# Moving the second heads' scaled copy of a row into the place of the next head's raw bias values

## The chip, the cores and the metric

The kernel runs on one core of a Trainium2 chip. The metric is the device time of one execution in microseconds. Lower is better. The core's engines are called as in the profile: PE (TensorE matmul), PEld (its weight loads), DVE (VectorE), ACT (ScalarE), POOL (GpSimd) and SP (SyncE, which here only issues DMAs). Each engine works through its own queue in order and waits there for what the others owe it.

## The reference, cut to what matters

One encoder layer on 1024 tokens of width 1024, all in float32. A combined projection feeds two kinds of attention heads. Group A is eight sliding-window heads. Group B, the "second heads", is eight heads of neighbourhood attention on a 16 x 64 grid of tokens: each token attends to a window of 8 x 16 tokens, with a learned bias for every offset in two dimensions.

```python
def row(args):                                   # one grid row of queries, group B
    q_r, r = args
    rs = jnp.clip(r - kh // 2, 0, rows - kh)
    k_rows = lax.dynamic_slice_in_dim(kg, rs, kh, axis=1)
    v_rows = lax.dynamic_slice_in_dim(vg, rs, kh, axis=1)
    ...
    bias = rpb32[:, row_off][:, :, col_off]
    s = jnp.einsum('bchd,bicjhd->bhcij', q_r, k_win) * scale + bias[None]
    p = jax.nn.softmax(s.reshape(B, B_HEADS, GRID_W, kh * NA_KW), axis=-1)
    return jnp.einsum('bhcij,bicjhd->bchd', p, v_win)
```

Behind both groups stand a norm of each group, an output projection with a residual, a gated MLP with a depthwise convolution, and a final norm.

## The kernel before

The tokens of the grid are put in an order in which a second head has eight blocks of 128 queries, called rows 0 to 7 here, and each block attends to itself and its neighbours: 384 keys, or 256 for rows 0 and 7. The heads are called 0 to 7. PE's order is written out by hand: between the matmuls of attention stand those of the projections and of the output projection of group A (the "filler", tiles `pj`), and the scores of a row are made two to three pairs of rows ahead of their use. The other engines' order is set by a scheduler from priorities and from which buffer is free.

A row goes through these steps. PE makes scores (L439). DVE adds the bias tile `xb` and takes the extreme, into a buffer `p` (L469). ACT takes the exponential and its sum (L473), and DVE the reciprocal `sm` (L474). From there a row takes one of two paths, by the string `QQTQQQTQ` of `PATH_B`:

- Rows 2 and 6 are T rows: POOL scales `p` in place (L477), PE transposes it (L501), ACT and DVE split the result into two float16 parts in the tile `turned` (L504, L505).
- The six others are Q rows: ACT writes the scaled high part into a staging tile, `hl` or one of two called `stage` (L488); POOL makes a scaled copy `y` (L493) and subtracts the high part from it, into the staging tile (L494); SP issues a DMA that transposes both parts into `turned` (L495, called the flip).

PE then multiplies `turned` with the values (L604); row 4's tile is first used in the chunk that follows the transposes of row 6.

The bias tile of the next head is begun at row 4 of the head before. A DMA on SP loads the raw values `rr` (L551), and two POOL operations turn them and the mask into `xb` (L562, L563). `rr` has one buffer of 489 float32 values per partition. POOL may do this no earlier than row 2's L477 ("scaled"). The pool `p` has six buffers; before the change it holds both the probability tiles `p` and the copies `y`, so that a Q row takes two of the six. POOL also subtracts the high parts of projection weights (L157, tile `wlo`).

Of the kernel before, what the change touches and what calls it, by code (L numbers as in the profile page):

```python
# [13 lines left out]
F32 = mybir.dt.float32  # L14
# [23 lines left out]
TURNED, PS, HLS, SPARE_A, LOWS = 3, 6, 1, (2, 5), 1  # L38
# [13 lines left out]
RAW_LEN = RPB_W * (ROWS - 1) + 24  # L52
# [11 lines left out]
def hybrid_layer(tc, xT, w_in, w_out, w_gate, w_up, w_down, small, sink, rpb, consts, rope, out):  # L64
    nc = tc.nc
    with ExitStack() as ctx:
# [8 lines left out]
        apool = inner("att", 2)  # L75
# [367 lines left out]
        apart = lambda ap: ap.rearrange("p (c w) -> p c w", w=128)  # L443
# [3 lines left out]
        def staged():  # L447
            if not stage:
                t = big("stage", "op").bitcast(F16)
                stage.extend(apool.tile([128, 3, 2, 128], F16, name="hl", tag=f"hl{i}", bufs=1) for i in range(HLS))  # L450
                stage.extend(t[:, 768 * i:768 * i + 768].rearrange("p (c s w) -> p c s w", s=2, w=128) for i in range(2))
            stage.append(stage.pop(0))
            return stage[-1]

        class Rows:
# [5 lines left out]
            def softmax(self, path, j, ps, n, bias, nsink=None, skip=0):  # L461

                c = n // 128
                with tc.high_priority(offset=50):
                    p = apool.tile([128, 386], F32, name="p", tag="p", bufs=PS)
                    nm, sm = (spool.tile([128, 1], F32, name=x) for x in ("nm", "sm"))
                    if nsink is not None:
                        nc.gpsimd.tensor_copy(p[:, n:n + 1], nsink)
                    nc.vector.tensor_tensor_reduce(  # L469
                        out=apart(p[:, 0:n]), in0=apart(ps[:, 0:n]), in1=bias, scale=1.0, scalar=3e38 if nsink is None else nsink,  # L470
                        op0=ALU.add, op1=ALU.min, accum_out=nm)
                    e = n if nsink is None else n + 1
                    nc.scalar.activation(p[:, 0:e], p[:, 0:e], AF.Exp, bias=nm, scale=-1.0, accum_out=sm)  # L473
                    nc.vector.reciprocal(sm, sm)  # L474
                    x = apart(p[:, 0:n])
                    if path in "PT":
                        mark["scaled"] = nc.gpsimd.tensor_scalar(x, x, sm, P_TOP, op0=ALU.mult, op1=ALU.mult)  # L477
                    if path == "T":
                        return lambda: self.turn(j, p, c, skip)
                    hl = staged()  # L480
                    hi, lo = (hl[:, 0:c, s] for s in range(2))
                    if path == "P":
                        nc.scalar.activation(hi, x, AF.Copy)
                        nc.gpsimd.tensor_tensor(lo, x, hi, op=ALU.subtract)
                    else:
                        by = spool.tile([128, 1], F32, name="by")
                        nc.vector.tensor_scalar(by, sm, P_TOP, None, op0=ALU.mult)
                        nc.scalar.activation(hi, x, AF.Copy, scale=by)  # L488
                        if path == "D":
                            nc.vector.scalar_tensor_tensor(lo, x, by, hi, op0=ALU.mult, op1=ALU.subtract)  # L490
                        else:
                            y = apart(apool.tile([128, 384], F32, name="y", tag="p", bufs=PS, padded_shape=[128, 386])[:, 0:n])
                            nc.gpsimd.tensor_scalar(y, x, sm, P_TOP, op0=ALU.mult, op1=ALU.mult)  # L493
                            nc.gpsimd.tensor_tensor(lo, y, hi, op=ALU.subtract)  # L494
                    mark["flip"] = nc.sync.dma_start(self.tile[:, j, skip:skip + c].rearrange("p i s q -> p (i s) q"), hl[:, 0:c], transpose=True)  # L495
# [1261 lines left out]
        for i, (p, j, c) in enumerate(order):  # L1757
# [4 lines left out]
            f, n = PARTS[c]  # L1762
# [148 lines left out]
```

## Time and profile before

| | |
|---|---|
| time, median of 3 runs | 1028.34 us (1028.22 to 1029.49) |
| time of the profiled execution | 1027.81 us |
| its span, first to last instruction | 1026.0 us |
| mean granted TensorE clock | 0.997 |
| PE busy | 1009.7 us (98%) |
| DVE busy | 875.6 us (85%) |
| ACT busy | 676.3 us (66%) |
| POOL busy | 216.4 us (21%) |
| second heads on PE, first to last use of `turned` | 190 to 344 us of the span |

The time of an execution is a little longer than its span, by 1.8 us here. PE is busy nearly all the time, so what the kernel takes is what PE does plus what PE waits. POOL's share is low over the whole span, but nearly all of its work lies in the first third, where the heads are. The change concerns the stretch of the second heads alone, from 186 to 346 us.

### The profile page before, as it was taken

Reading aid. Unit: us, or ns where it says so; the run is one execution under the profiler, and the core shown is the slowest. Engines: PE = TensorE matmul, PEld = TensorE weight load, DVE = VectorE, ACT = ScalarE, POOL = GpSimd, SP = SyncE. Lnnn points to the kernel's source line nnn. Section 1 sums busy time; section 2 is a strip of 40 time slices with the busy share of each in tenths; the row PEclk is TensorE's granted clock in tenths of the full one; section 3 lists DMA queues with packets and bytes.
Section 4 is the critical chain, followed back from the end, with each engine's and each line's share of the span. In section 5 each row is a group of like instructions: output and inputs, shape, how many; then the busy total and the mean of one; then the engine's idle time right before and its main releaser. Section 6 shows DMA issues by size and latency. Waiting matters only on the chain.

```text
span 1026.0 us, 15565 instructions
## 1 busy us (share of the span) xinstructions
PE 1009.7 (98%) x5102; PEld 577.8 (56%) x5102; DVE 875.6 (85%) x1714; ACT 676.3 (66%) x1242; POOL 216.4 (21%) x339
## 2 busy tenths in 40 slices
PE   9999999999999999999999999999999999999997
PEld 7877777777775545544444444444444444444446
DVE  6799988767898899999897988788888888999875
ACT  8667787768687687645777777754634666655551
POOL 2235455877866210001000000000000000000002
PEclk9999999999999999999999999999999999999998
DMA  8556564787799875201787767633232788978744
GB/s 314 198 133 139 115 138 106 159 155 137 136 195 216 280 255 171 82 1 42 251 279 251 266 230 256 232 114 134 82 114 103 256 263 291 309 245 269 250 147 165
DMA packets 143938, 191.79 MB, mean 187 GB/s; under 512 B 77360, under 2 KB 88112, under 8 KB 143856
## 3 DMA queue, kind: packets, MB, share of 16 engines
q1 hardware_dynamic: 133264, 164.84, 55.9%
q10 hardware_dynamic: 10592, 25.95, 6.6%
q8 instruction: 40, 0.66, 0.3%
q14 instruction: 42, 0.34, 0.1%
HBM read 132.81 MB, written 28.57 MB: 157 GB/s over the span
## 4 chain that ended last, share of the span: by engine, by line
PE 65%; DVE 2%; DMA 1%; ACT 1%; issue 0%; POOL 0%; DVEq 0%; ACTq 0%; POOLq 0%
PE dn L1199 6%; PE dn L1200 6%; PE dn L1201 6%; PE pj L180 6%; PE z L1200 5%; PE z L1201 5%; PE z L1199 5%; PE y L1200 4%; PE y L1201 4%; PE y L1199 4%; PE x L1199 4%; PE x L1200 4%; PE x L1201 4%; PE ss L1239 1%; DMA turned<-stage 1%; DVE wlo L1174 0%
## 5 line engine op out<-in xcount | busy, mean ns | idle before, releaser
L1201 PEld LDWEIGHTS <-wlo 128*128 128x128 f16 x898 | 87.8, 98 | 101.2
L1199 PEld LDWEIGHTS <-whi 128*128 128x128 f16 x898 | 88.0, 98 | 100.3
L1200 PEld LDWEIGHTS <-whi 128*128 128x128 f16 x898 | 87.8, 98 | 100.3
L1201 PE MATMUL dn<-xd,wlo 128*128 128x512 f16 (+1 forms) x330 | 120.5, 365 | 0.0
L1200 PE MATMUL dn<-xd,whi 128*128 128x512 f16 (+1 forms) x330 | 120.5, 365 | 0.0
L1199 PE MATMUL dn<-xd,whi 128*128 128x512 f16 (+1 forms) x330 | 120.5, 365 | 0.0
L172 PE MATMUL pj<-xgh,whi 128*128 128x512 f32 x248 | 106.9, 431 | 0.0
L1201 PE MATMUL z<-hg,wlo 128*128 128x512 f16 x264 | 100.2, 379 | 0.0
L1199 PE MATMUL z<-hg,whi 128*128 128x512 f16 x264 | 100.2, 379 | 0.0
L1200 PE MATMUL z<-hg,whi 128*128 128x512 f16 x264 | 100.2, 379 | 0.0
L174 PE MATMUL pj<-xgh,wlo 128*128 128x512 f32 x248 | 97.7, 394 | 0.0
L173 PE MATMUL pj<-xgl,whi 128*128 128x512 f32 x248 | 97.6, 393 | 0.0
L473 ACT ACTIVATE p<-p,nm 128x385 f32<-128x385 f32 (+3 forms) x128 | 74.7, 584 | 34.6 <-DVE nm L469 28.6
L1173 ACT ACTIVATE whi<-ws,m 128x512 f16<-128x512 f32 (+1 forms) x96 | 65.8, 708 | 37.7 <-DVE ws L1340 22.9
L1174 DVE SCALAR_TENSOR_TENSOR wlo<-ws,m,whi 128x512 f16<-128x512 f32 (+1 forms) x96 | 70.3, 742 | 18.3 <-ACT whi L1173 18.1
L1054 POOL TENSOR_TENSOR back<-back,cst 128x4 f32<-128x4 f32 (+1 forms) x7 | 2.8, 395 | 356.8 <-DVE back L1053 356.8
L1188 ACT ACTIVATE scan<-scan 128x1024 f32<-128x1024 f32 (+1 forms) x60 | 61.1, 1018 | 18.4 <-DMA scan<-in_w_down_dram 13.2
L1173 ACT ACTIVATE whi<-raw,m 128x512 f16<-128x512 f32 (+1 forms) x78 | 51.1, 699 | 16.8 <-DMA raw<-in_w_down_dram 10.1
L1174 DVE SCALAR_TENSOR_TENSOR wlo<-raw,m,whi 128x512 f16<-128x512 f32 (+1 forms) x78 | 55.5, 733 | 6.7 <-ACT whi L1173 6.6
L1201 PE MATMUL y<-hg,wlo 128*128 128x512 f16 x160 | 60.7, 379 | 0.0
L1200 PE MATMUL y<-hg,whi 128*128 128x512 f16 x160 | 60.7, 379 | 0.0
L1199 PE MATMUL y<-hg,whi 128*128 128x512 f16 x160 | 60.7, 379 | 0.0
(296 smaller groups left out, 2464.7 us busy)
## 6 DMA issues: line engine op xcount, KB each, us to landing
xd<-x SPq DMA_DIRECT2D x77, 256.0 KB, 5.3
raw<-in_w_down_dram SPq DMA_DIRECT2D x64, 256.0 KB, 3.3
x<-c ACTq DMA_DIRECT2D x22, 512.0 KB, 4.2
scan<-in_w_gate_dram SPq DMA_DIRECT2D x18, 512.0 KB, 4.7
scan<-in_w_up_dram SPq DMA_DIRECT2D x18, 512.0 KB, 5.5
raw<-in_w_gate_dram SPq DMA_DIRECT2D x18, 512.0 KB, 3.5
raw<-in_w_up_dram SPq DMA_DIRECT2D x18, 512.0 KB, 3.6
raw<-in_w_in_dram SPq DMA_DIRECT2D x32, 256.0 KB, 3.2
```

The source lines that it names most:

```text
L172: nc.tensor.matmul(ps, w[0], x[0][:, tsl(h)], start=first, stop=False)
L173: nc.tensor.matmul(ps, w[0], x[1][:, tsl(h)], start=False, stop=False)
L174: nc.tensor.matmul(ps, w[1], x[0][:, tsl(h)], start=False, stop=last)
L180: nc.tensor.matmul(ps, a, b, start=i == 0 and b is x[h][0] and a is w[0], stop=i == len(ws) - 1 and a is w[1])
L473: nc.scalar.activation(p[:, 0:e], p[:, 0:e], AF.Exp, bias=nm, scale=-1.0, accum_out=sm)
L1173: mark["whi"] = nc.scalar.activation(hi, src, AF.Copy, scale=by)
L1174: nc.vector.scalar_tensor_tensor(lo, src, by, hi, op0=ALU.mult, op1=ALU.subtract)
L1188: nc.scalar.activation(t, t, AF.Square, accum_out=dst)
L1199: nc.tensor.matmul(ps, w[0], x[0], start=first and i == 0, stop=False, skip_group_check=True)
L1200: nc.tensor.matmul(ps, w[0], x[1], start=False, stop=False, skip_group_check=True)
L1201: nc.tensor.matmul(ps, w[1], x[0], start=False, stop=last and i == len(ws) - 1, skip_group_check=True)
L1239: nc.tensor.matmul(narrow[h][:, c:c + 1], s2[:, c * 128:(c + 1) * 128], ones[:, 0:1], start=c == 0 and d == ADDED[h] - 1, stop=d == KT - 1 ...
```

## The change

The copy `y` of a Q row of the second heads no longer comes from the six buffers of the pool `p`. It takes the single buffer `rr`, padded to that buffer's length, which between two heads holds the raw bias values.

```diff
                         else:
-                            y = apart(apool.tile([128, 384], F32, name="y", tag="p", bufs=PS, padded_shape=[128, 386])[:, 0:n])
+                            y = apart(apool.tile([128, 384], F32, name="y", tag="rr", bufs=1, padded_shape=[128, RAW_LEN])[:, 0:n])
                             nc.gpsimd.tensor_scalar(y, x, sm, P_TOP, op0=ALU.mult, op1=ALU.mult)
                             nc.gpsimd.tensor_tensor(lo, y, hi, op=ALU.subtract)
```

Since the buffer is one, its tenants follow each other in the order in which the program asks for it: the copies of rows 0, 1 and 3 of a head, then the raw values of the next head, then the copies of rows 4, 5 and 7. PE's order is the same row for row. POOL, SP, DVE and ACT have the same instructions in another order.

On POOL, head 4, before: behind row 2's L477 come the bias tile, row 3, row 4 and row 5, one weight part, and row 6's L477.

```order
L477 TENSOR_SCALAR p<-p,sm 128x384 [waits DVE_49]
L562 TENSOR_TENSOR xb<-cst,rr 128x384 [waits DMAHW0_49]
L563 TENSOR_TENSOR xb<-cst,rr 128x2x128
L493 TENSOR_SCALAR y<-p,sm 128x384 [waits DVE_49]
L354 TENSOR_TENSOR gains<-par,up 128x1 [waits DVE_49]
L908 TENSOR_TENSOR gains<-gains,mix_up 128x4 [waits Pool_49]
L494 TENSOR_TENSOR stage<-y,stage 128x3x128 [waits DMAHW1_49,Activation_49]
L493 TENSOR_SCALAR y<-p,sm 128x384 [waits DVE_49]
```

After:

```order
L477 TENSOR_SCALAR p<-p,sm 128x384 [waits DVE_49]
L493 TENSOR_SCALAR y<-p,sm 128x384 [waits DVE_49,Pool_49]
L354 TENSOR_TENSOR gains<-par,up 128x1 [waits DVE_49]
L908 TENSOR_TENSOR gains<-gains,mix_up 128x4 [waits Pool_49]
L494 TENSOR_TENSOR stage<-y,stage 128x3x128 [waits DMAHW0_49,Activation_49]
L562 TENSOR_TENSOR xb<-cst,rr 128x384 [waits DMAHW7_49]
L563 TENSOR_TENSOR xb<-cst,rr 128x2x128
L493 TENSOR_SCALAR y<-p,sm 128x384 [waits DVE_49,Pool_49]
```

The bias tile has moved from ahead of row 3 to between row 3 and row 4. Behind these rows follow, in both, the rest of row 4 and row 5, the weight part, and row 6's L477. In head 5 that L477 stands between row 4's L493 and L494 after the change.

On SP, head 4, before: the raw values for head 6 are asked for as soon as the bias tile of head 5 is made, ahead of the flips of rows 3 and 4.

```order
L551 DMA rr<-in_rpb_dram 128x1x489 [waits Pool_49]
L495 DMA_TRANSPOSE turned<-stage 128x6x128 [waits DMAHW0_49,PE_49,Pool_49]
L495 DMA_TRANSPOSE turned<-stage 128x6x128 [waits DMAHW1_49,PE_49,Pool_49]
L382 DMA_TRANSPOSE v<-vhl 128x16x64 [waits DMAHW2_49,DVE_49]
L382 DMA_TRANSPOSE v<-vhl 128x16x64 [waits DMAHW3_49]
```

After:

```order
L495 DMA_TRANSPOSE turned<-stage 128x6x128 [waits PE_49,Pool_49]
L551 DMA rr<-in_rpb_dram 128x1x489 [waits DMAHW7_49]
L382 DMA_TRANSPOSE v<-vhl 128x16x64 [waits DMAHW0_49,DVE_49]
L382 DMA_TRANSPOSE v<-vhl 128x16x64 [waits DMAHW1_49]
L495 DMA_TRANSPOSE turned<-stage 128x6x128 [waits DMAHW2_49,PE_49,Pool_49]
```

The load of the raw values for head 5 itself now stands right behind row 3's flip. In head 3 the load stands ahead of row 3's flip and waits for POOL itself.

On DVE the scores of the next row (L469) have moved ahead of small or bulk work in several places, because a `p` buffer is free earlier. In head 5, before:

```order
L474 RECIPROCAL sm<-sm 128x1 [waits Activation_49]
L201 TENSOR_TENSOR mg<-mixa,mg 128x2x512
L487 TENSOR_SCALAR by<-sm 128x1 [waits DVE_49]
L469 ISA p,nm<-s,xb 128x384 [waits PE_49]
L469 ISA nm 128x1
```

After:

```order
L474 RECIPROCAL sm<-sm 128x1 [waits Activation_49]
L469 ISA p,nm<-s,xb 128x384 [waits PE_49,Pool_49]
L469 ISA nm 128x1
L487 TENSOR_SCALAR by<-sm 128x1 [waits DVE_49]
L201 TENSOR_TENSOR mg<-mixa,mg 128x2x512
```

Row 4's scores are read ahead of L201, which splits a tile of group A's output for the projection.

## The prediction

> **What bounds the kernel now.** I read the page first, then the stretch of the second heads by windows, then PE's waits in it, then the rows of POOL, PE and SP around row 4 of each head.
>
> ```profile
> PE 1009.7 (98%) x5102; PEld 577.8 (56%) x5102; DVE 875.6 (85%) x1714; ACT 676.3 (66%) x1242; POOL 216.4 (21%) x339
> 186.00:346.00 160.00, 157.82 (x894) 115.30 (x893) 124.56 (x354) 114.21 (x254) 116.94 (x143) 1.00 0.82 167
> PE o L604 <- DMA turned<-stage: 1.1, 2, 0.9
> PE o L604 <- DMA turned<-hl: 0.5, 1, 0.5
> PE pt L501 <- POOL p L477: 0.4, 1, 0.4
> ```
>
> PE bounds the kernel. In the stretch that the change touches it is busy 157.8 of 160 us, and its waits are 2.2 us, nearly all for finished rows. So there is at most 2.2 us to gain here, and every microsecond that a row comes later than PE's hand-written order asks for it is lost in full: PE's order is the same after the change, and the stages behind are PE's too. POOL is the fuller neighbour: 116.9 of 160 us.
>
> **What the change removes and adds.** No instruction is added. Six copies per head (48 in all) leave the pool `p`. That gives DVE a free `p` buffer earlier. In PE's waits above none is for DVE's reading of scores, so the removal is worth at most a part of the 2.2 us; DVE's new order brings row 4 of head 5 forward past one L201, and I count this inside the lag below.
>
> What it adds is one chain per head, for heads 0 to 6. Before, the raw values of a head were in place a whole head early, and the bias tile cost POOL only its own two operations. Now the raw values may be loaded only when row 3's subtraction has read the copy that stands in their place, and row 4's copy may be made only when the bias tile has read the raw values. POOL works in order, so it stands still meanwhile with rows 4, 5 and 6 behind it. The prices, one step after the other:
>
> ```profile
> L495 SPq DMA_TRANSPOSE turned<-stage x31: 1188/1220/1982, 190.2 to 339.7; - x31
> DMA to landing us min/median/max: 2.4/3.4/5.7
> rr<-in_rpb_dram SPq DMA_DIRECT2D x8, 244.5 KB, 4.7
> DMA to landing us min/median/max: 4.3/4.7/5.9
> L562 POOL TENSOR_TENSOR xb<-cst,rr x8: 979/986/1515, 38.9 to 313.0; 128x384 f32<-128x384 f32 x8
> L563 POOL TENSOR_TENSOR xb<-cst,rr x8: 707/734/1697, 39.9 to 314.0; 128x256 f32<-128x256 f32 x8
> L493 POOL TENSOR_SCALAR y<-p,sm x48: 474/584/1555, 181.1 to 338.5; 128x384 f32<-128x384 f32 x32, 128x256 f32<-128x256 f32 x16
> L494 POOL TENSOR_TENSOR stage<-y,stage x31: 668/913/1494, 189.2 to 339.0; 128x384 f16<-128x384 f32 x16, 128x256 f16<-128x256 f32 x15
> L477 POOL TENSOR_SCALAR p<-p,sm x16: 577/586/1110, 186.4 to 337.9; 128x384 f32<-128x384 f32 x16
> ```
>
> The first landing row is that of the flips, the second that of the raw values. From the end of row 3's subtraction: 1.3 us in which SP issues row 3's flip (1.22) and turns to the load; 4.7 to its landing; 1.7 for the bias tile (0.99 + 0.73); 1.5 for row 4 (0.58 + 0.91); 1.5 for row 5; 0.6 for row 6's L477. Together 11.3 us to the end of L477, and 9.2 to the end of row 4's subtraction, which a flip of 3.4 us follows. In head 3 the load goes ahead of the flip: 1.3 less.
>
> How long PE leaves for that is read from where row 3's subtraction ends and where PE transposes row 6 now (heads 0 to 6 in order):
>
> ```profile
> 189.22 0.92 POOL L494 TENSOR_TENSOR stage<-y,stage 128x384 f16<-128x384 f32 x1
> 198.65 0.49 PE L501 MATMUL pt<-cst,p 128*128 128x128 f32 x3
> 208.75 0.93 POOL L494 TENSOR_TENSOR stage<-y,stage 128x384 f16<-128x384 f32 x1
> 219.90 0.49 PE L501 MATMUL pt<-cst,p 128*128 128x128 f32 x3
> 228.96 0.92 POOL L494 TENSOR_TENSOR stage<-y,stage 128x384 f16<-128x384 f32 x1 [0.34 <-POOL y L493]
> 241.14 0.49 PE L501 MATMUL pt<-cst,p 128*128 128x128 f32 x3
> 251.17 1.33 POOL L494 TENSOR_TENSOR stage<-y,stage 128x384 f16<-128x384 f32 x1
> 263.51 0.49 PE L501 MATMUL pt<-cst,p 128*128 128x128 f32 x3
> 274.74 1.49 POOL L494 TENSOR_TENSOR stage<-y,stage 128x384 f16<-128x384 f32 x1
> 285.39 0.49 PE L501 MATMUL pt<-cst,p 128*128 128x128 f32 x3
> 297.22 0.93 POOL L494 TENSOR_TENSOR stage<-y,stage 128x384 f16<-128x384 f32 x1 [0.45 <-POOL y L493]
> 305.09 0.55 PE L501 MATMUL pt<-cst,p 128*128 128x128 f32 x3
> 305.48 0.49 PE L604 MATMUL o<-turned,v 128*128 128x256 f16 x4
> 315.34 0.91 POOL L494 TENSOR_TENSOR stage<-y,stage 128x384 f16<-128x384 f32 x1
> 323.35 0.55 PE L501 MATMUL pt<-cst,p 128*128 128x128 f32 x3 [0.44 <-POOL p L477]
> 323.74 0.49 PE L604 MATMUL o<-turned,v 128*128 128x256 f16 x4
> ```
>
> PE's lead, from the end of the subtraction to the transposes: 8.5, 10.2, 11.3, 11.0, 9.2, 6.9, 7.1 us. The bias tile no longer stands ahead of row 3, which gives something back: nothing where row 3 waits for DVE, at most the tile's own time where it does not. What bounds it are the rows of DVE's reciprocal for row 3, after which POOL could have begun:
>
> ```profile
> 206.44 0.15 DVE L474 RECIPROCAL sm<-sm 128x1 f32<-128x1 f32 x1
> 228.03 0.58 POOL L493 TENSOR_SCALAR y<-p,sm 128x384 f32<-128x384 f32 x1 [0.49 <-DVE sm L474]
> 249.95 1.14 POOL L493 TENSOR_SCALAR y<-p,sm 128x384 f32<-128x384 f32 x1 [0.72 <-DVE sm L474]
> 272.31 0.15 DVE L474 RECIPROCAL sm<-sm 128x1 f32<-128x1 f32 x1
> 272.94 0.58 POOL L493 TENSOR_SCALAR y<-p,sm 128x384 f32<-128x384 f32 x1
> 280.89 1.73 POOL L157 TENSOR_TENSOR wlo<-raw,whi 128x512 fp32r<-128x512 f32 x1
> 294.58 0.15 DVE L474 RECIPROCAL sm<-sm 128x1 f32<-128x1 f32 x1
> 295.22 1.55 POOL L493 TENSOR_SCALAR y<-p,sm 128x384 f32<-128x384 f32 x1
> 313.14 0.17 DVE L474 RECIPROCAL sm<-sm 128x1 f32<-128x1 f32 x1
> 314.67 0.58 POOL L493 TENSOR_SCALAR y<-p,sm 128x384 f32<-128x384 f32 x1
> ```
>
> Given back: head 1 1.1 (206.6 to the start at 207.7), heads 2 and 3 nothing, head 4 0.5, head 5 0.5, head 6 1.3. Head 0 gets 0.4, my estimate, since a weight part now stands between row 3's copy and its subtraction.
>
> Head by head, with what the new order puts into the chain:
> - Head 0: 11.3 + 0.3 (a small operation, L901) - 0.4 - 8.5 = 2.7 us of waiting.
> - Head 1: row 6's L477 now stands ahead of row 5's subtraction: 11.3 - 0.9 - 1.1 - 10.2 is below zero. Nothing.
> - Head 2: one weight part stands ahead of L477; at the 1.3 of the undisturbed ones (estimate, the 1.73 above being a slow one): 11.3 + 1.3 - 11.3 = 1.3.
> - Head 3: 11.3 - 1.3 - 11.0: nothing.
> - Head 4: 11.3 + 1.7 (L157 as in its row) - 0.5 - 9.2 = 3.3.
> - Head 5: L477 stands ahead of row 4's subtraction, so PE's transposes wait 1.3 + 4.7 + 1.7 + 0.6 + 0.6 - 0.5 - 6.9 = 1.5 us only. But row 4's tile is wanted by the third matmul of the row at 305.48, about 305.7. Its subtraction ends 9.2 + 0.6 - 0.5 = 9.3 us after 298.15 - that is 307.5 - and its flip lands at 310.9: 5.2 us late in all.
> - Head 6: by the transposes 11.3 - 1.3 - 7.1 = 2.9; by row 4's flip 316.25 - 1.3 + 9.2 + 3.4 = 327.6 against about 324.0 wanted, 3.6. Against this, PE's wait of 5 us in head 5 lets DVE catch up: there DVE reads scores some 2 to 4 us after PE made them, and PE's wait shortens that lag by up to 1.7 us (my estimate). I take 2.8.
>
> The waits of earlier heads don't reduce those of later ones up to head 4, because there rows follow PE: a late PE makes row 3 late by as much. Sum 2.7 + 1.3 + 3.3 + 5.2 + 2.8 = 15.3 us. PE's own 2.2 us of waits in this stretch lie mostly in heads 5 to 7 and vanish under the new ones: -2.2. That leaves +13.1.
>
> Costed at nothing: the weight parts (L157) behind the stall, since two of them now run inside it, and the loads behind the flips in SP's queue (next heads' keys and queries, weights), wanted a head later. Row 7 and the next head's rows 0 and 1 are late at first, but POOL has idle time between heads to catch up (43 us of 160). If that cover is gone, the second rival below comes in.
>
> [...]
>
> **The rivals.**
>
> *Hidden.* PE's lead covers the chain after all, and the freed `p` buffers save up to the 2.2 us: 1025.6 to 1027.8 us. It decides if the chain takes no longer than 7 us to L477, so that the load would have to land in under 1 us. The landing row speaks against it. This is the rival on the other side.
>
> *A short load.* The load lands as quickly as the fastest row of its size:
>
> ```profile
> h1d<-h ACTq DMA_DIRECT2D x16, 256.0 KB, 2.2
> ```
>
> [...] Those are writes to memory; the raw values are gathered in overlapping pieces. [...]
>
> *Compounding.* The high part of a Q row goes into one of three staging tiles, so ACT may write row 0 of the next head only when row 4's flip has landed. ACT is in order and has exponentials behind it: with row 4's flip 5 to 6 us late, ACT stands 2 to 3 us per head, DVE behind it, and row 3 of the next head starts late. That adds 2 us in six heads: about 1053. For it: heads 4 to 6, where DVE is already late. Against it: ACT and PE stand at the same time, and ACT is busy only 114 of 160 us.
>
> **How the numbers follow.** Against the profiled execution (1027.81 us, span 1026.0) the sum gives 1040.9; the median of the runs is 0.5 above that execution, so I say 1041. Ends: with the load at 4.3, the flips at 2.4 and all of the lag regained, heads 0, 2, 4, 5, 6 wait 2.3, 0.9, 2.9, 3.8, 0.8, less 2.2: 1037. If the two weight parts also fall into the stall, 1034. With the load at 5.9 five heads wait 1.2 more and heads 1 and 3 a little, POOL's operations in heads 4 to 6 run at their slow durations (1.5 to 1.7 us in place of 0.6 to 1.0, about 1 us a head), and nothing of the 2.2 is regained: 1053. Chances: this forecast 0.75, compounding 0.12, a short load 0.05, hidden 0.08, of which 0.05 within 0.2% (2 us, about what a measurement of this kernel can tell from no change) and 0.03 faster. Slower is the forecast, compounding and the short load: 0.92. The range 1033 to 1051 leaves out the short load, the hidden case and a part of compounding.
>
> **What would show it.** In the profile after: L562 on POOL idle for 3 to 6 us before it, released by the DMA of `rr`, in each of heads 0 to 6; the load issued 1.2 to 2 us after row 3's subtraction ends; PE waiting at L501 for L477 in heads 0, 2 and 4 and at L604 for a flip in heads 5 and 6; PE's busy time in the stretch unchanged; everything from 346 us on shifted and otherwise the same. The prediction is wrong if POOL's idle time before L562 is short, if POOL's late rows find PE not yet there, or if ACT's L488 shows long waits for flips.

## Result and profile after

The changed kernel takes 1056.07 us (median of 6 runs, 1055.6 to 1059.4) against 1028.28 for the kernel before (6 runs). The ratio is 1.0274, 95% interval 1.0259 to 1.0289. It is slower by 27.8 us; the forecast was 13. The profiled execution is the longest of the six: 1059.4 us, span 1057.6, against 1027.81 and 1026.0 before.

First the page: PE's busy time, and the row of PE's granted clock in 40 slices.

```profile
PE 1018.2 (96%) x5102; PEld 582.1 (55%) x5102; DVE 874.2 (83%) x1714; ACT 677.6 (64%) x1242; POOL 212.1 (20%) x339
PEclk9999999998989899999999999999999999999998
```

The span is 31.6 us longer. PE's busy time grew by 8.5 (1018.2 against 1009.7), with the same 5102 matmuls; its idle time grew by 23.1 (39.4 against 16.3). The 8s in slices 10, 12 and 14 of the clock row were not there before. The windows of the stretch (span, PE, PEld, DVE, ACT, POOL busy with counts, PEclk, DMA share, GB/s) show the same:

```profile
186.00:346.00 160.00, 143.06 (x761) 105.90 (x759) 106.84 (x304) 100.40 (x220) 97.68 (x120) 0.95 0.67 143
346.00:376.00 30.00, 24.70 (x143) 14.77 (x144) 17.90 (x52) 16.02 (x36) 15.46 (x23) 0.89 0.64 161
```

In the first 160 us PE does 761 matmuls in place of 894, and every other engine has become less busy too: nobody is overloaded, all wait for one another. The waits of PE, POOL, DVE and ACT from 170 to 376 us (us in all, times, longest) say in what order:

```profile
PE pt L501 <- POOL p L477: 19.3, 6, 5.9
PE o L604 <- DMA turned<-stage: 2.9, 1, 2.9
POOL xb L562 <- DMA rr<-in_rpb_dram: 19.4, 3, 7.2
POOL xb L562 <- DVE mixa L886: 6.2, 1, 6.2
POOL xb L562 <- DVE tm L248: 5.1, 1, 5.1
POOL xb L562 <- DVE kb L332: 2.5, 1, 2.5
DVE p L469 <- POOL xb L563: 7.3, 5, 2.4
DVE wo_by L248 <- POOL wo_by L902: 6.6, 1, 6.6
ACT stage L488 <- DMA turned<-stage: 10.1, 5, 3.5
```

PE stands 19.3 us for row 6's L477 and 2.9 us for a flip, 22.2 in all. POOL stands ahead of L562, the bias tile, for the load of the raw values. (The three rows that name DVE are the same kind of wait: in the trace the load's last semaphore update is at 195.30, 243.87 and 292.58 us there, and L562 begins 0.07 us behind it, as it does where the row names the DMA.) Two rows were not in my forecast: DVE now waits for the bias tile, at the first rows of the next head, and once for a small POOL operation behind the stalled one (L902). The last row, ACT's waits for flips, is what the prediction named as a sign of being wrong: 10.1 us in place of 0.7 before.

The chain of head 2, from POOL's, SP's and PE's rows (start, duration, engine, line; some rows between are left out):

```profile
236.79 0.93 POOL L494 TENSOR_TENSOR stage<-y,stage 128x384 f16<-128x384 f32 x1 [1.17 <-PE pt L501]
238.08 1.95 SPq L495 DMA_TRANSPOSE turned<-stage  x1
240.09 0.60 SPq L551 DMA_DIRECT2D rr<-in_rpb_dram  x1
243.94 0.98 POOL L562 TENSOR_TENSOR xb<-cst,rr 128x384 f32<-128x384 f32 x1 [2.48 <-DVE kb L332]
246.36 0.91 POOL L494 TENSOR_TENSOR stage<-y,stage 128x384 f16<-128x384 f32 x1
248.91 1.26 POOL L157 TENSOR_TENSOR wlo<-raw,whi 128x512 fp32r<-128x512 f32 x1
250.15 0.59 POOL L477 TENSOR_SCALAR p<-p,sm 128x384 f32<-128x384 f32 x1
250.79 0.90 PE L501 MATMUL pt<-cst,p 128*128 128x128 f32 x3 [4.30 <-POOL p L477]
```

Row 3's subtraction ends at 237.72; the flip and the load are issued; the bias tile starts 3.9 us after the load; L477 ends at 250.74, and PE, ready since 246.49, starts 0.05 us later. Here is the same for every head, beside what the prediction had. "Chain" is from the end of row 3's subtraction to the end of row 6's L477, "lead" from the same start until PE is ready for the transposes; PE's wait at the transposes is chain less lead, within 0.1 us, and nothing where the lead is longer.

| head | chain forecast, measured | lead forecast, measured | PE's wait forecast, measured |
|---|---|---|---|
| 0 | 11.6, 12.8 | 8.9, 10.5 | 2.7, 2.35 |
| 1 | 10.4, 10.9 | 11.3, 8.9 | 0, 2.08 |
| 2 | 12.6, 13.0 | 11.3, 8.8 | 1.3, 4.30 |
| 3 | 10.0, 9.7 | 11.0, 12.4 | 0, 0 |
| 4 | 13.0, 14.7 | 9.7, 11.0 | 3.3, 3.78 |
| 5 | 8.9, 9.1 | 7.4, 8.3 | 5.2 (most for a flip), 0.94 and 2.91 for the flip |
| 6 | 11.3, 13.8 | 8.4, 8.0 | 2.8, 5.87 |

The chain came within 0.5 us in heads 1, 2, 3 and 5, and was 1.2, 1.7 and 2.5 us longer than forecast in heads 0, 4 and 6. The lead was 2.4 and 2.5 us shorter than I reckoned in heads 1 and 2, and 0.9 to 1.6 longer in heads 0, 3, 4 and 5. So the waits of heads 0 and 4 came near by luck: chain and lead were both too short by about as much.

### The profile page after: what moved, and what is told of

Its sections match the earlier page's. It is cut to its first block, busy times and chain, and to the rows that moved or that the text cites. A ratio compares the mean times of both kernels' runs of the same rounds, so it can differ in the third digit from the quotient of the medians.

```text
span 1057.6 us, 15620 instructions
## 1 busy us (share of the span) xinstructions
PE 1018.2 (96%) x5102; PEld 582.1 (55%) x5102; DVE 874.2 (83%) x1714; ACT 677.6 (64%) x1242; POOL 212.1 (20%) x339
## 4 chain that ended last, share of the span: by engine, by line
PE 70%; DVE 11%; DMA 6%; issue 5%; POOL 4%; ACT 4%; SPq 0%; ACTq 0%; POOLq 0%; DVEq 0%
PE pj L180 7%; PE dn L1201 6%; PE dn L1199 6%; PE dn L1200 6%; PE z L1199 4%; PE z L1200 4%; PE z L1201 4%; PE y L1200 3%; PE x L1199 3%; PE y L1201 3%; PE x L1200 3%; PE x L1201 3%; PE y L1199 3%; PE pj L172 2%; DVE p L469 2%
## 5 line engine op out<-in xcount | busy, mean ns | idle before, releaser
L1199 PEld LDWEIGHTS <-whi 128*128 128x128 f16 x898 | 88.1, 98 | 100.2
L1199 PE MATMUL dn<-xd,whi 128*128 128x512 f16 (+1 forms) x330 | 120.4, 365 | 0.0
L1199 PE MATMUL z<-hg,whi 128*128 128x512 f16 x264 | 100.1, 379 | 1.4 <-DVE gs L1395 1.4
L1199 PE MATMUL y<-hg,whi 128*128 128x512 f16 x160 | 60.6, 379 | 0.0
```

The costliest lines, as they stand in the source:

```text
L1199: nc.tensor.matmul(ps, w[0], x[0], start=first and i == 0, stop=False, skip_group_check=True)
```

## Experiments

Diffs are against the changed kernel unless said otherwise; ratios are to the kernel before on the same chip.

### e1: a buffer of the copies' own

```diff
-TURNED, PS, HLS, SPARE_A, LOWS = 3, 6, 1, (2, 5), 1
+TURNED, PS, HLS, SPARE_A, LOWS = 3, 5, 1, (2, 5), 1
-  y = apart(apool.tile([128, 384], F32, name="y", tag="rr", bufs=1, padded_shape=[128, RAW_LEN])[:, 0:n])
+  y = apart(apool.tile([128, 384], F32, name="y", tag="yy", bufs=1)[:, 0:n])
```

> The copy y gets one buffer of its own and the probability pool has five buffers in place of six, so the bytes are those of after; raw bias values keep their own buffer. Theory A (the loss comes from the raw load waiting for row 3's copy and holding back row 4): no POOL wait before the bias tile, clock as before, 1026 to 1030 us. Rival B (the loss comes from taking the copies out of the pool and the order that DVE and ACT get by it): stays above 1045 us.

Measured: 1027.41 us, ratio 0.9987 (0.9978 to 0.9996).

```profile
186.00:346.00 160.00, 158.13 (x896) 115.54 (x895) 122.52 (x353) 114.67 (x254) 116.19 (x142) 1.00 0.83 167
```

In the same stretch PE does 896 matmuls, at full clock. So neither the single buffer of the copies nor their leaving the six costs anything; the whole loss comes from sharing the place with the raw values.

### e2: no load of the raw values

```diff
-            nc.sync.dma_start(raw, src)
+            nc.gpsimd.memset(raw, 0.0) if h else nc.sync.dma_start(raw, src)
```

> After, with the load of the raw values of heads 1 to 7 replaced by a clear of the buffer on POOL: these heads' learned bias is left out. The order of tenants in the buffer and the place of the bias tile between rows 3 and 4 stay. Theory A: the 6 us in which the load is issued and lands are the chain; with 0.4 us in their place PE's waits fall to what they were, 1027 to 1032 us, clock 0.997. Rival C (the bias tile's later place is enough, since DVE waits for it at the next head's row 0): above 1038 us.

Measured: 1029.5 us, ratio 1.0009 (0.9996 to 1.0022). This kernel leaves out the learned bias of heads 1 to 7. The sharing and the late place of the bias tile are still there; only the load in the middle of the chain is gone, and with it all but about 1 us of the loss.

### e10: the load ahead of row 3's flip

```diff
-            nc.sync.dma_start(raw, src)
+            with tc.high_priority(offset=300):
+                nc.sync.dma_start(raw, src)
```

> The changed kernel with the load of the raw values ahead of row 3's flip on the DMA queue in every head, in place of behind it (in head 3 it stands there already). Theory M (the waits come from the chain behind row 3's subtraction, link by link): each of the six other heads' chains is shorter by 1.2 to 1.3 us, row 3's own flip has that much to spare in most heads; the sum of TensorE's waits falls from 22 to 15 to 17 us, and the time to 1046 to 1051. Rival N (the late rows are set by DVE's and ACT's lag, not by the load): 1054 to 1058.

Measured: 1045.72 us, ratio 1.0164 (1.0149 to 1.018). PE's waits in its trace (lines behind the edit are one higher):

```profile
PE pt L501 <- POOL p L477: 10.2, 5, 3.5
186.00:346.00 160.00, 144.53 (x790) 106.67 (x789) 112.61 (x324) 104.25 (x232) 107.09 (x132) 0.98 0.73 154
```

The waits for row 6 fall from 19.3 to 10.2 and the half-clock time from 23.9 to 6.8 us. A link of 1.2 to 1.3 us in six heads, some 7.5 us, was worth 10.4 in the medians. Theory M holds and N does not: the load is a link of what PE waits for. The time is even a little below M's range.

### e6 and e7: the chain in every second head

```diff
-  y = apart(apool.tile([128, 384], F32, name="y", tag="rr", bufs=1, padded_shape=[128, RAW_LEN])[:, 0:n])
+  y = apart(apool.tile([128, 384], F32, name="y", **(dict(tag="rr", bufs=1, padded_shape=[128, RAW_LEN])
+            if self.h in (0, 2, 4, 6) else dict(tag="p", bufs=PS, padded_shape=[128, 386])))[:, 0:n])
```

In e7 the heads are (1, 3, 5). (Cut: a row also keeps the number of its head, in `h`.)

> Only heads 0, 2, 4 and 6 put their copies in the place of the raw values; in heads 1, 3, 5 and 7 the copy takes one of the six probability buffers as before. Theory H (head 2's 4.3 us and head 6's 5.9 us of waiting are partly brought over from the head ahead, whose bias tile came late and held DVE at the next head's first row): with no late bias tile ahead of them, heads 0, 2, 4, 6 wait 2.4, 1.3, 3.3, 2.8 as in my sum, about 10 us in all, one or two dips of the clock, 1034 to 1042. Rival J (each head's wait is its own, and my terms for heads 2 and 6 were simply too small): 2.4, 4.3, 3.8, 5.9, 16.4 us, three dips of the clock, 1046 to 1052.

> Only heads 1, 3 and 5 put their copies in the place of the raw values. Theory H (the waits of heads 1 and 5 contain what the head ahead brought): head 1 waits 0, head 3 0, head 5 4 to 5 us, one dip of the clock at most, 1030 to 1034. Rival J (each head's wait is its own): head 1 waits 2.1, head 3 0, head 5 3.9, 1032 to 1036. The times overlap; head 1's wait in the trace tells them apart.

Measured: e6 1048.55 us, ratio 1.0192 (1.0175 to 1.0209); e7 1040.06 us, 1.0099 (1.0079 to 1.0118). In e6 heads 0, 2, 4, 6 wait 2.08, 2.14, 2.81 and 4.77 us for row 6. In e7 head 1 waits 0 and head 5 waits 2.67 for row 6 and 2.33 for a flip. Head 2 tells what was carried over. These are the end of row 3's scores on PE and the start of their reading on DVE, first in the kernel before, then in the changed one, then in e6, where the head ahead has no chain:

```profile
224.99 0.34 PE L439 MATMUL s<-kb,q 128*128 128x384 f32 x1
226.07 0.56 DVE L469 CUSTOM_DVE_ANT_0 p<-s,xb 128x384 f32<-128x384 f32 x1
```

```profile
230.16 0.34 PE L439 MATMUL s<-kb,q 128*128 128x384 f32 x1
233.37 0.56 DVE L469 CUSTOM_DVE_ANT_0 p<-s,xb 128x384 f32<-128x384 f32 x1
```

```profile
228.48 0.34 PE L439 MATMUL s<-kb,q 128*128 128x384 f32 x1
229.55 0.56 DVE L469 CUSTOM_DVE_ANT_0 p<-s,xb 128x384 f32<-128x384 f32 x1
```

DVE begins 0.7 us after the scores are made in the kernel before, 2.9 us in the changed one, and 0.7 in e6. With that, the lead of head 2 is back from 8.8 to 10.6 and its wait halves. In head 1 the wait is gone altogether in e7. So heads 1 and 2 wait for what the chain of the head ahead had made late, as theory H has it; whether it was the bias tile that held DVE, as H says too, these two runs don't tell. Head 6 waits 4.77 with no chain ahead of it: there my own term was too small, as rival J has it.

Both times miss H's ranges. In e6 PE also stands 2.9 us for a weight part (L157) that the new order puts behind a stalled POOL. In e7 head 6, which has no chain, waits 5.1 us, 4.2 of them for flips (the first row, less the 2.33 of head 5) and 0.85 at scores:

```profile
PE o L604 <- DMA turned<-stage: 6.6, 3, 3.7
PE pt L501 <- POOL p L477: 2.7, 1, 2.7
ACT whi L167 <- DMA raw<-in_w_out_dram: 4.3, 2, 3.9
```

The last row shows one way in which lateness can travel: SP issued a weight load at 324.1, right behind two flips, and ACT stood 3.9 us for it with exponentials and a row's high part behind. How much of that the flips made was not tried. The two halves of the change cost 20 and 11.5 us, 31.4 together, against 27.8 for the whole: a chain in the next head does not make the loss more than the sum.

### e9: the chain at row 0

```diff
-                    if b == 4 and h < 7:
+                    if b == 0 and h < 7:
```

> The changed kernel, but the next head's raw values are loaded and turned into the bias tile ahead of row 0 of a head in place of row 4: the sharing and the chain stay, and only their place in the head moves, to where TensorE's lead is largest (in the kernel before, row 1's subtraction in heads 1 to 4 ends 7.8 to 10.4 us ahead of its use, in head 6 4.7). Theory K (what costs is that the chain stands where the lead is short, and that the bias tile is then late for the next head's first row): from the end of row 7's subtraction 7.7 us to the end of the bias tile, 3.1 for rows 0 and 1, 3.4 for the flip, 14.2 in all against 12.2, 14.3, 14.5, 15.9, 12.0 and 9.3 us to the use of rows 0 and 1 of heads 1 to 6: waits of 2.0, 0, 0, 0, 2.2 and 4.9, 9 us, one or two dips of the clock, and DVE's waits for a bias tile gone: 1035 to 1043. Rival L (any place costs as much, since POOL stands 5 us a head either way): 1050 to 1058.

Measured: 1048.5 us, ratio 1.0198 (1.0179 to 1.0218), between the two ranges.

```profile
PE pt L501 <- POOL p L477: 7.8, 4, 4.3
PE o L604 <- DMA turned<-hl: 6.1, 5, 2.1
```

DVE's wait for a bias tile is gone, as K says. But PE now waits at row 2's transposes (the 7.8 us), in heads 3 to 6: row 2's L477 stands on POOL behind rows 0 and 1, and I had priced only the flips of those two. The place matters, and this one is not free either.

### e4: the output projection's scales later

```diff
-        SCAN_OUT_AT, OUT_SCALES_AT = [], (8, 3)
+        SCAN_OUT_AT, OUT_SCALES_AT = [], (10, 3)
```

> After, with the small chain of output scales (POOL L901, L902, then DVE L248) placed two projection tiles later, out of head 0's stall. Theory F (DVE stood 6.7 us in head 0 for POOL's L902 behind the stall, which made heads 1 and 2 late): PE's waits in heads 1 and 2 fall from 2.1 and 4.3 to about 0 and 1.5, one clock dip less: 1048 to 1052 us. Rival G (heads 1 and 2 are late from the bias tile alone): 1054 to 1057 us.

Measured: 1055.62 us, ratio 1.026 (1.0244 to 1.0276). DVE's wait for L902 falls from 6.6 to 1.8 us, and the waits of heads 0 and 1 for row 6 fall by 2.0 us, but the time stays where it was: head 4 waits 0.5 longer and one new wait of 0.9 us appears. In head 1, ACT now stands 3.50 us for the flip of head 0's row 4, where in the changed kernel it stood for DVE, so that half of that head's wait is left. Taking away DVE's wait alone is worth next to nothing.

### e3 and e5: PE kept busy while it waits

```diff
-                for i in range(c):
+                for i in range(-busy, c): nc.tensor.matmul(ps[:, 0:128], ones, ones, start=True, stop=True) if i < 0 else \
```

with `busy` as the expectations say, for row 6 of heads 0 to 6. (Cut: how the number reaches this loop.)

> After, with small matmuls of a constant on PE (16, 14, 30, 0, 28, 6, 40 in heads 0 to 6) right ahead of row 6's transposes, to fill about the time that PE stood there (2.4, 2.1, 4.3, 0, 3.8, 0.9, 5.9 us). Theory D (a PE that stands loses granted clock, and 8.5 us of the loss is matmuls at half clock): granted clock 0.995 or more, none or one stretch at 0.5, 1046 to 1050 us. Rival E (the waits are all, the clock costs nothing that counts): 1055 us or more.

> The changed kernel with 8, 6, 14, 0, 12, 3, 18 extra 128x128 matmuls ahead of row 6's transposes in heads 0 to 6: in e3 each pair of passes kept TensorE 0.23 us, twice what was reckoned, so its 16, 14, 30, 0, 28, 6, 40 held the transposes back by 1.6, 2.7, 3.4, 0, 2.0, 0.4 and 2.9 us after L477 had ended. Theory D (the half clock after the long waits costs time of its own, about 8 us of busy time, and the extra matmuls of e3 gave that back by overshooting): clock 0.995 or more, the transposes held back by under 0.5 us in each head, 1046 to 1051. Rival (the half clock costs nothing, since rows then come late by as much less or more and the end is set by the rows): clock as high, 1054 to 1058.

Measured: e3 1061.39 us, ratio 1.031 (1.0296 to 1.0325); e5 1062.21 us, 1.032 (1.0301 to 1.0338). Of e3 the page's row, of e5 the waits:

```profile
PE 1040.2 (98%) x5370; PEld 608.4 (58%) x5370; DVE 872.3 (82%) x1714; ACT 677.3 (64%) x1242; POOL 211.2 (20%) x339
PE pj L174 <- POOL wlo L157: 4.5, 1, 4.5
```

In e3 the clock is back (0.996) and PE has 17 us of idle time, about as before, but the extra matmuls took 30.5 us of PE, and ran past the end of L477 by 13 us in all. In e5 they are fewer, but the extra instructions had changed POOL's order around head 2, where PE now stood 4.5 us for a weight part and lost its clock after all (0.990). Neither isolates the clock. How much of the 8.5 us of extra busy time would come back at full clock stays open.

### e11 and e12: made waits where PE is the bound

Against the kernel before, in the late stages (e11: six places, two POOL operations each; e12: two places, seven each):

```diff
         def group(ps, ws, xs, first, last):
+            seen[0] += first
+            if first and seen[0] in (20, 32, 44, 56, 68, 80):
+                nc.tensor.matmul(ps[:, 0:128], ones, jam[:, 0:128], start=True, stop=True)
+                for _ in range(2):
+                    nc.gpsimd.tensor_scalar(jam, jam, 0.5, None, op0=ALU.mult)
+                nc.tensor.matmul(ps[:, 0:128], ones, jam[:, 0:128], start=True, stop=True)
```

> The kernel before with six made waits of TensorE in the late stages, where it is the bound and has next to no idle time (0.55 us in 624): each is a pair of small matmuls with two POOL operations of 0.58 us between them, so that the second matmul waits about 1.5 us. Theory D (a wait that leaves a 3.41 us window over 60% idle makes the next window run at half clock; shorter ones do not): 9 us of waits and 1.5 to 3.3 of the twelve small matmuls, no dip: 1038 to 1041. Rival (any wait drops the clock): six dips of 1.7 us more, 1048 to 1052.

> The kernel before with two made waits of TensorE in the late stages, with seven POOL operations each, about 4.5 us a wait: as much waiting as in e11, in longer pieces. Theory D: 9 us of waits, 0.5 to 1.1 of the four small matmuls, and one or two windows at half clock behind each, 1.7 us lost in each window: 1041 to 1046, and the clock's loss in the profile (half of the time at half clock) is found in the time in full. Rival (the half clock costs nothing here): 1037 to 1039.

Measured: e11 1064.25 us, ratio 1.0351 (1.0335 to 1.0366); e12 1051.77 us, 1.0235 (1.0218 to 1.0252). Of e11 the page, the waits and the POOL operation; two windows, with the first wait and behind it; then e12's waits and page.

```profile
PE 1024.7 (96%) x5126; PEld 584.9 (55%) x5126; DVE 879.0 (83%) x1714; ACT 678.3 (64%) x1242; POOL 237.8 (22%) x352
PE y L1206 <- POOL jam L1205: 14.1, 4, 3.8
PE dn L1206 <- POOL jam L1205: 5.8, 2, 3.1
L1205 POOL TENSOR_SCALAR jam<-jam x12: 1169/1482/2222, 522.7 to 939.7; 128x384 f32<-128x384 f32 x12
522.20:525.80 3.60, 0.37 (x3) 0.18 (x1) 3.56 (x4) 3.34 (x7) 3.05 (x2) 1.00 0.60 187
525.80:529.30 3.50, 2.95 (x8) 1.44 (x9) 1.85 (x4) 2.98 (x5) 0.50 (x1) 0.51 0.80 187
```

```profile
PE 1014.4 (96%) x5110; PEld 580.0 (55%) x5110; DVE 877.7 (83%) x1714; ACT 678.0 (64%) x1242; POOL 235.9 (22%) x354
PE y L1206 <- POOL jam L1205: 11.1, 1, 11.1
PE z L1206 <- POOL jam L1205: 9.2, 1, 9.2
```

The window and the share in theory D are those of the changed kernel's trace: up to its last 11 us, a window of 3.41 us at full clock with 1.77 us of idle time on PE (52%) or less was followed by full clock, one with 2.11 (62%) or more by half. The sizes I had expected are wrong: the POOL operation took 1.2 to 2.2 us in place of 0.58, so that e11's "short" waits were 2.8 to 3.8 us each and all six were followed by half clock (0.51 from 525.8 to 529.3 us behind the first). The two sums of waiting came out nearly equal, 19.9 and 20.3 us, and yet e11 is slower, by 12.5 us in the medians and 8.6 in the spans of the profiled executions (1062.2 and 1053.6). PE's busy time explains it: 15.0 above the kernel before in e11, 4.7 in e12. Both executions had 23.9 us at half clock (their last 7 us left out), but PE was busy in 22.5 of them in e11 and in 9.3 in e12, where most of these windows fell inside the wait itself and there was nothing to slow down. Half of the difference, 6.6 us, is the clock; the 16 small matmuls that e11 has more, at some 0.3 us, fit the rest of the 10. PE's idle time grew by no less than the made waits, by 21.2 and 22.9 us, so nothing of the half clock was taken back: in these stages it is paid in full, and six waits of 3 us cost more than two of 10.

### e8: two buffers of the copies' own

`PS` is 4, and the copies have `tag="yy", bufs=2`.

> The copies get two buffers of their own, and the probability buffers are four in place of six; the raw values keep their place to themselves. If buffers of the copies' own are what helps, as one buffer with five probability buffers gave 0.9987: 1026 to 1028.5. If four probability buffers are too few: DVE waits for a free one before L469 and rows come late, 1029 to 1040.

Measured: 1026.91 us, ratio 0.9982 (0.9973 to 0.9992). Like e1, it is a little faster than the kernel before, at the edge of what can be told apart: four probability buffers are enough once the copies have places of their own.

## Why the prediction was right and wrong

Against the profiled execution the forecast was 1040.9, and it took 1059.4: 18.5 us short (15 by the medians), from three places: PE's waits 6.9, PE's busy time 8.5, idle time elsewhere 3.1.

- *The mechanism* was right. The load was issued 1.3 to 2.4 us after the subtraction (head 3 at once), and the bias tile began 3.6 to 5.8 us after that. PE waited as named in heads 0, 2, 4 and 5; head 6 waited at the transposes and not for a flip, and head 1, where I had nothing, waited too. e1 and e2 show that this is the whole loss. "Hidden" and "a short load" are out: from the load's issue to the start of its reader it took 3.6 to 5.8 us, where the row quoted for the short load has 2.2 to the landing.
- *The step that failed first* is "The waits of earlier heads don't reduce those of later ones up to head 4, because there rows follow PE". In heads 1 and 2 they add to them: these heads lost 2.4 and 2.5 us of lead, and 0 became 2.08, 1.3 became 4.30. e6 and e7 take the head ahead out, and the waits fall to 2.14 and 0. How the lateness was carried is read from the trace, and it is not the same in both. In head 1, DVE stood 6.65 us for L902, until 202.00; the bias tile had been ready since 197.03. In head 2 it was ACT. First row 1's scores being read on DVE in the kernel before, then DVE's and ACT's rows in the changed one:

```profile
219.66 0.55 DVE L469 CUSTOM_DVE_ANT_0 p<-s,xb 128x384 f32<-128x384 f32 x1
```

```profile
222.07 0.43 DVE L469 CUSTOM_DVE_ANT_1 p<-s,xb 128x256 f32<-128x256 f32 x1 [2.08 <-POOL xb L563]
224.04 0.55 DVE L469 CUSTOM_DVE_ANT_0 p<-s,xb 128x384 f32<-128x384 f32 x1
226.60 0.51 ACT L488 ACTIVATE stage<-p,by 128x256 f16<-128x256 f32 x1 [3.46 <-DMA turned<-stage]
227.54 0.60 ACT L473 ACTIVATE p<-p,nm 128x384 f32<-128x384 f32 x1
228.27 0.16 DVE L474 RECIPROCAL sm<-sm 128x1 f32<-128x1 f32 x1 [2.54 <-ACT p L473]
```

  DVE's wait for the bias tile had been made up by row 1: its scores are read 4.4 us later than before, and PE itself had by then waited 4.4 us. But ACT stood 3.46 us for the flip of head 1's row 4 before it could write row 0's high part, so that row 1's exponential began 2.9 us after its scores had been read, and DVE stood 2.54 us for it. That is the rival of compounding, to which I had given 0.12, by the way that it names. Its size was not right: it asked for 2 us in six heads, and in heads 3 to 5 the lead was longer than reckoned, so that its 1053 is near by luck. No run takes away ACT's wait alone; that it is what made head 2 late is read from this trace only, and which part of the 10.1 us reached PE in other heads was not told apart.
- *Head 6's term was mis-sized:* 2.8 forecast, 5.87 measured, and 4.77 in e6 without a chain in head 5. The chain there is 13.8 us in place of 11.3, from these rows:

```profile
344.63 2.02 POOL L562 TENSOR_TENSOR xb<-cst,rr 128x384 f32<-128x384 f32 x1 [7.23 <-DMA rr<-in_rpb_dram]
346.62 0.70 POOL L563 TENSOR_TENSOR xb<-cst,rr 128x256 f32<-128x256 f32 x1
351.30 0.90 PE L501 MATMUL pt<-cst,p 128*128 128x128 f32 x3 [5.87 <-POOL p L477]
```

The bias tile began 5.75 us after the load's issue at 338.88, where the sum had 4.7: the slow end of the row that I had quoted. The tile itself took 2.7 us in place of 1.7; L562's 2.02 lies beyond its row's longest, 1.52. With head 5 at 3.85 in place of 5.2, head 0 at 2.35 and head 4 at 3.78, PE's waits are 22.2 in place of 15.3: 6.9 of the 18.5 us.

- *"PE's busy time in the stretch unchanged" is the second step that failed*: 8.5 us. I took the waits at their own length, with PE's work at full clock behind them. In this execution the clock stood at half for 23.9 us in and behind the waits of heads 2, 4, 5 and 6. PE was busy in 16.4 of them, and half of that, 8.2 us, is nearly the whole 8.5. The slowest of the six runs of the changed kernel, 1059.4 us, also has the lowest clock, 0.985; among the others, with 0.987 to 0.990 and 1055.6 to 1056.3 us, no order shows. e11 and e12 show that such a loss is real where PE is the bound (PE's busy time up by 15.0 and 4.7 us); how much of it the late rows would have eaten here is open, as said.
- The last 3.1 us are idle time of PE outside the chain; 2.5 of it lie behind 376 us, at L1199 and L1032, and I have no cause for them.

The 2.2 us of earlier waits did vanish as reckoned.

## What to carry to other kernels

When a buffer is shared between a loaded value and a working copy, the load can no longer run ahead: price it as a chain from the last reader of the one to the first use of the other, and then ask who else waits for what comes late at its end, in the next round too: here ACT for a staging tile and DVE for a small operation behind the stall. When PE must wait, add to the wait the matmuls behind it at half clock: in the changed kernel half clock began inside each of the waits of 2.91, 3.78, 4.30 and 5.87 us and held for 3.41 to 6.83 us, and the waits of 2.35 and 2.08 us brought none; in e6 one of 2.08 us did (0.51 from 200.7 to 204.1 us). A buffer of its own, taken from a pool with one or two to spare, cost nothing here (ratios 0.9987 in e1 and 0.9982 in e8).

## What the runs showed of the hardware

In the clock record of the changed kernel's trace, full clock begins at 6.25 us. Half clock stands from 248.60 to 255.42, from 299.80 to 306.62, from 327.10 to 330.52, from 347.58 to 354.41 and from 1050.73 us to the end. Each of these changes lies a whole number of 3.41 us behind the first (71 times to 248.60, 306 times to 1050.73). In the kernel before, half clock begins 297 times 3.41 us behind the first full clock (5.92 and 1019.68 us).

Counted in windows of that length, these are the windows at full clock in which PE was idle for 1.0 us or more in the changed kernel:

| windows begin at, us | PE idle in 3.41 us | clock of the next window |
|---|---|---|
| 74.52, 153.02, 197.40, 221.29, 388.54, 852.76 | 1.01, 1.33, 1.69, 1.77, 1.33, 1.02 | 1.00 |
| 245.18, 296.38, 323.69, 344.17 | 2.11, 2.41, 2.65, 2.16 | 0.50 |
| 1047.32 | 1.33 | 0.50 |

The last one doesn't fit: around the small matmuls at the very end (L233, L266), 1.33 us of idle time were followed by half clock, and so they were in the kernel before (the window at 1016.26, also 1.33 us). So idle time as the profile counts it does not decide alone, and what else does was not tried. Within the stretches at half clock up to 354.41 us, the four windows with 0.30 us idle or less were followed by full clock, the three with 1.37, 2.19 and 3.41 us by another window at half clock. A near pair at full clock, from e6 and from e10 (windows, PE busy first), 1.79 us idle followed by full clock and 1.97 by half:

```profile
292.90:296.30 3.40, 1.61 (x8) 1.00 (x6) 3.08 (x6) 2.37 (x6) 3.22 (x5) 1.00 0.30 59
296.30:299.70 3.40, 2.38 (x15) 1.92 (x16) 2.29 (x5) 1.95 (x6) 3.23 (x5) 1.00 0.52 134
```

```profile
291.60:295.00 3.40, 1.43 (x9) 0.91 (x8) 3.40 (x8) 2.18 (x5) 3.40 (x4) 0.99 0.62 126
295.00:298.40 3.40, 3.40 (x13) 2.37 (x12) 0.84 (x4) 1.31 (x3) 2.95 (x6) 0.50 0.34 92
```

In e6 PE was idle for 1.79 and 1.02 us of the two windows, 2.81 together, as long as head 4's wait, and the second ran at full clock; in e10 1.97 us inside one window, 58% of its 3.40, were followed by half clock.

A POOL operation of one kind and size (TENSOR_SCALAR, 128x384 float32) took 0.58 us in the second heads (L493, median) and 1.2 to 2.2 us in the late stages (L1205 of e11). What made it slower there was not tried.
